# A second block inversion emitted in pieces among the joins and scan steps, and two kinds of stores issued by GpSimd

## The chip, the cores and the metric

The kernel runs on one core of a Trainium2 chip. A core has five engines that run their own instruction streams in order: TensorE (PE in the profile; its weight loads are PEld), VectorE (DVE), ScalarE (ACT), GpSimd (POOL) and SyncE (SP), which here does nothing but issue transfers. Transfers run on the core's 16 DMA engines whichever engine issues them. The metric is the device time of one execution in microseconds (us), and lower is better.

## The reference

One layer of a bidirectional encoder is applied to two sequences of 1024 and 256 tokens, with width 1024 and all in float32. Three groups of heads read one projection of the normalised input: six heads of a gated delta rule, six of retention, four of window attention. The part that the change touches is the delta rule, run once forwards and once backwards in time, in chunks of 64 tokens:

```python
a_mat = jnp.einsum('nbhcd,nbhsd->nbhcs', k_beta, k) * gamma
t_mat = jnp.where(strict, a_mat, 0.0) + jnp.eye(CHUNK, dtype=q.dtype)
rhs = jnp.concatenate([v * beta[..., None], k_beta * jnp.exp(decay)[..., None]], axis=-1)
sol = lax.linalg.triangular_solve(t_mat, rhs, left_side=True, lower=True, unit_diagonal=True)
...
def step(state, inp):
    u_c, w_c, qk_c, qd_c, kd_c, cd_c = inp
    v_new = u_c - jnp.einsum('bhcd,bhde->bhce', w_c, state)
    o = jnp.einsum('bhcd,bhde->bhce', qd_c, state) + jnp.einsum('bhcs,bhse->bhce', qk_c, v_new)
    state = state * cd_c + jnp.einsum('bhcd,bhce->bhde', kd_c, v_new)
    return state, o
```

Each chunk and head needs the inverse of a 64x64 unit triangular matrix; then a scan carries a 64x64 state per head from chunk to chunk.

## The kernel before

The 1280 tokens are 10 blocks of 128, that is 20 chunks of 64. The program runs in five stages; the first and the last are not touched.

1. Load and normalise the input, project the delta rule's queries and keys, convolve them (up to about 180 us).
2. **Preparation** (`prep_stream`, L584 to L643). It walks the blocks from 9 down to 0, and each block has two halves, d = 0 and 1 for the two directions. A half loads a small table `dj` (L606, issued by GpSimd), multiplies it with `sd` on TensorE (L610), exponentiates on ScalarE (`ge`, L613 and L616), and multiplies the products of keys and queries (`gram`, in the two `sa` buffers of PSUM) by it on VectorE: the matrix to invert (`at`, L624) and the step's three matrices (`l2`, printed as `l`, L626 to L628). GpSimd copies a column (`elc`, L629). Then come stores to DRAM: four of `agd` (L631), one of `ad` (L633), and four of `l2d` (L635 and, three times, L638). The next half's `dj` is loaded one block ahead.
3. **Inversion** (`invert(g)`, L402 to L429). Group 1 holds blocks 9 to 5 and is done first; group 0 holds blocks 4 to 0. Two loads (L405) bring the group's 32x32 diagonal blocks, 120 of them per direction, into rows 0 and 1 of the tile `ot`; one long product on VectorE (L414, 120x2048, printed `ot<-ot`) and 60 short ones (L423, L424) invert them all at once; two stores of `yd` (L429), in pieces of 32 numbers, bring them out. Both groups use the same two rows of `ot`, so group 0 can be loaded when group 1 is stored.
4. **Joins and scan** (`scan_stream`, L767 to L791). A `join` (L668) loads two 32x32 inverses (`yn`) and the block between them (`an`), multiplies them on TensorE and stores the 64x64 inverse; there are four for each group. Steps of the scan (L711) follow, one per chunk and direction; the four joins of group 0 come at step 2 (`JN`).
5. In the meantime `fill` (L1107) brings attention, retention and further products of the input with the weights to TensorE.

A weight product is emitted in pieces of 512, 512 and 256 tokens (`dense`, L174), 24 matmuls each: 8 blocks of width times three terms of a split into two parts. During preparation 13 of these products are spread among its halves by weight: `spread` (L443) advances the stream that is behind in proportion to its length. During stage 4 `weave` (L431) does the same by the numbers that the streams yield. Eight of the products are gates (L469): their piece goes through a copy (`sz`) and three more operations on ScalarE and one on VectorE (`sg`), and six of them are stored by SyncE (`gd`, L477), with one buffer for each of the two tiles.

What the streams emit is only a wish. The framework's scheduler simulates the engines and sets the order on each from the order of emission and what is ready there. So a change of emission moves instructions on all engines, far from the lines that changed. On the chip each engine then follows its order strictly; an instruction that waits holds all behind it.

Of the kernel before, what the change touches and what calls it, by code (L numbers as in the profile page):

```python
# [36 lines left out]
PP = ["x0", "x1", "x2", 6, 7, 3, "cq0", "cq1", "ck", "cv", 4, 0, 5]  # L37
PB = [1, 2, "q0"]
RS = [["k0", "v0"], ["q1"], ["k1", "v1"], ["k2"], ["v2"], ["q2"], []]
T_PREP = 10.0  # L40
# [13 lines left out]
def encoder_kernel(ctx: ExitStack, tc: tile.TileContext, I, O, dbg=None, upto=99):  # L54
    nc = tc.nc
# [32 lines left out]
    def tt(eng, out, a, b, op):  # L88
        eng.tensor_tensor(out=out, in0=a, in1=b, op=op)  # L89
# [30 lines left out]
    ot = big.tile([128, 8, PADW], F32, tag="OT", name="ot")  # L120
# [257 lines left out]
    L2D = [[tc.dram_tile([2, 128, 3, 3, 64], F32, name=f"l2d{d}_{b}") for b in range(NB)] for d in range(2)]  # L378
# [3 lines left out]
    YDD = [[tc.dram_tile([120, 32, 32], F32, name=f"yd{d}_{g}") for g in range(2)] for d in range(2)]  # L382
# [5 lines left out]
    T, B = slice(0, 64), slice(64, 128)  # L388
# [11 lines left out]
    IREG = (0, 1)  # L400

    def invert(g):  # L402
        for d in range(2):
            with tc.high_priority():
                nc.sync.dma_start(out=ot[0:120, IREG[d], 0:1056].rearrange("p (a b) -> p a b", a=32),  # L405
                                  in_=AGD[d][g].rearrange("q c p r x -> (q c p) r x"))

        def two(o0, o1, *dims):

            a = ot[0:120, IREG[0], o0:o0 + 1]  # L410
            return bass.AP(a.tensor, a.offset, [list(a.ap[0]), [(IREG[1] - IREG[0]) * PADW + o1 - o0, 2], *([list(e) for e in dims])])

        y, yd = two(0, 0, (33, 32), (1, 32)), two(32, 32, (0, 32), (33, 32))
        tt(V, y, y, yd, MUL)  # L414
        yield 4.2
        for s in range(1, 31):
            na, nb = s, 31 - s
            t3 = two(1056, 1056, (nb, na), (1, nb))

            c = two(s, 33 * (32 - s) + 31 - s, (33, na), (0, nb))  # L420
            r = two(33 * s + s + 1, 33 * (31 - s), (0, na), (1, nb))
            o = two(s + 1, 33 * (32 - s), (33, na), (1, nb))
            tt(V, t3, c, r, MUL)  # L423
            tt(V, o, o, t3, ADD)  # L424
            if s % 3 == 0:
                yield 2.8
        V.memset(two(0, 0, (34, 32)), 1.0)
        for d in range(2):
            nc.sync.dma_start(out=YDD[d][g], in_=ot[0:120, IREG[d], 0:1056].rearrange("p (a b) -> p a b", a=32)[:, :, 0:32])  # L429

    def weave(*run):  # L431

# [10 lines left out]
    def spread(*run):  # L443

        run = [[0.0, t, g] for t, g in run]
        while run:
            q = min(run, key=lambda e: e[0])
            t = next(q[2], None)
            if t is None:
                run.remove(q)  # L450
            else:
                q[0] += t / q[1]
                yield t

    def length(ns):
        return 12.8 * len(ns) or 1.0, prods(*ns)
# [48 lines left out]
    with tc.tile_pool(name="pa", reuse_waits="tile", bufs=2) as pa:  # L505
# [78 lines left out]
        def prep_stream():  # L584
            for b in reversed(range(NB)):
# [18 lines left out]
                for d in range(2):  # L604
# [25 lines left out]
                    for q in range(4):  # L630
                        nc.sync.dma_start(out=AGD[d][b // 5][q, 2 * b % 10:2 * b % 10 + 2].rearrange("c p r x -> r (c p) x"),  # L631
                                          in_=at[32 * q:32 * q + 32, :, :, q % 2, :].rearrange("r c p x -> r (c p) x"))
                    nc.sync.dma_start(out=ADD_[d][b // 5][2 * b % 10:2 * b % 10 + 2].rearrange("c p q w t -> p c q w t"), in_=at)  # L633

                    nc.sync.dma_start(out=L2D[d][b][:, T].rearrange("r p a q t -> p r (a q t)"),  # L635
                                      in_=l2[T].rearrange("p r a q t -> p r (a q t)"))
                    for a, a2 in ((0, 1), (1, 0), (2, 2)):
                        nc.sync.dma_start(out=L2D[d][b][:, B, a2].rearrange("r p q t -> p r (q t)"),  # L638
                                          in_=l2[B, :, a].rearrange("p r q t -> p r (q t)"))
                    yield T_PREP / 2  # L640
                if b % 5 == 0:
                    assert "x2" in gone
                    yield from invert(b // 5)  # L643


        for _ in spread((10 * T_PREP + 2 * 32.2, prep_stream()), length(PP)):
            pass
    if upto <= 3:
        if dbg:
# [117 lines left out]
    def scan_stream():  # L767

        run = [list(range(16, 20)) + list(range(16)), list(range(15, -1, -1)) + list(range(19, 15, -1))]
        for d, cc in ((1, 5), (0, 5), (1, 0), (0, 0)):  # L770
            join(1, d, cc)
            yield T_JOIN
        done = {b: max(run[d].index(2 * b + r) for d in range(2) for r in range(2)) for b in range(NB)}
        for i in range(NC):
            if i == JN:
                for d, cc in ((0, 0), (1, 5), (0, 5), (1, 0)):
                    join(0, d, cc)
                    yield T_JOIN
                inv_cm.__exit__(None, None, None)
            for d in range(2):  # L780
                c = run[d][i]
                ends = (15, 19) if d == 0 else (0, 16)
                step(d, c, c in ((0, 16), (15, 19))[d], c in ends)
            yield T_STEP
            for b in FO:
                if done[b] == i - FD:
                    norm(b)
        for b in FO:
            if done[b] > NC - 1 - FD:
                norm(b)  # L790
        sp_cm.__exit__(None, None, None)  # L791
# [360 lines left out]
    with tc.tile_pool(name="fw", reuse_waits="tile", bufs=2) as fw:  # L1152
# [21 lines left out]
        for gi in range(2):  # L1174
            c0 = WSEQ[gi][1]
            w = wf.pop()
            for i, b in enumerate(range(NB) if gi else FO):
                tk = slice(b * 128, (b + 1) * 128)
                p = acc()
# [22 lines left out]
        for gi in range(2):  # L1202
# [10 lines left out]
            for b in range(NB):  # L1213
                tk = slice(b * 128, (b + 1) * 128)
                end = gi == 1 and b == NB - 1
                for j, (o, n) in enumerate(((0, 256), (256, 256)) if end else ((0, 512),)):
                    cs = slice(o, o + n)
                    p = acc()
# [50 lines left out]
```

## Time and profile before

| What | Value |
|---|---|
| Median of 3 runs | 1094.68 us (1089.72 to 1098.46) |
| Profiled execution, its own time | 1089.4 us |
| Its span | 1087.7 us |
| TensorE busy | 1012.3 us, 93% of the span |
| VectorE / ScalarE / GpSimd busy | 626.2 / 513.4 / 237.1 us |
| Transfers issued by SyncE | 118.97 MB |
| Transfers issued by GpSimd | 0.27 MB |

The busy share of an engine says that it had an instruction running. The granted clock of TensorE (PEclk) is the mean share of full speed; it is below 1 for some microseconds after TensorE sat idle, so that a stop costs its own length and a part of the work behind it. In timelines a bracket behind a row gives the engine's idle time just ahead of it, and what ended it. SPq rows are SyncE's issues of transfers; their time is how long the issue held the queue, not how long the data took.

### The profile page before, as it was taken

Reading aid. Unit: us, or ns where it says so; the run is one execution under the profiler, and the core shown is the slowest. Engines: PE = TensorE matmul, PEld = TensorE weight load, DVE = VectorE, ACT = ScalarE, POOL = GpSimd, SP = SyncE. Lnnn points to the kernel's source line nnn. Section 1 sums busy time; section 2 is a strip of 40 time slices with the busy share of each in tenths; the row PEclk is TensorE's granted clock in tenths of the full one; section 3 lists DMA queues with packets and bytes.
Section 4 is the critical chain, followed back from the end, with each engine's and each line's share of the span. In section 5 each row is a group of like instructions: output and inputs, shape, how many; then the busy total and the mean of one; then the engine's idle time right before and its main releaser. Section 6 shows DMA issues by size and latency. Waiting matters only on the chain.

```text
span 1087.7 us, 20998 instructions
## 1 busy us (share of the span) xinstructions
PE 1012.3 (93%) x7859; PEld 807.6 (74%) x7859; DVE 626.2 (58%) x1303; ACT 513.4 (47%) x1194; POOL 237.1 (22%) x406
## 2 busy tenths in 40 slices
PE   4999999999896799899998999989789999999996
PEld 4768878887785677677776777767567888888885
DVE  6666676754895985555555664575884333412333
ACT  8476779775454554444344322323341121534544
POOL 2001001111212210312323324554451000112311
PEclk9999999999898899999999899989989999999998
DMA  8112112777778336535544434464572530300211
GB/s 258 37 44 69 45 39 58 170 170 180 164 184 173 104 88 131 146 77 137 127 112 109 113 84 116 115 189 113 155 231 65 172 100 1 97 1 10 98 78 77
DMA packets 199071, 120.57 MB, mean 111 GB/s; under 512 B 105906, under 2 KB 180442, under 8 KB 198970
## 3 DMA queue, kind: packets, MB, share of 16 engines
q1 hardware_dynamic: 194074, 118.97, 40.9%
q8 instruction: 62, 1.02, 0.4%
q0 software_dynamic: 4896, 0.27, 0.4%
q14 instruction: 39, 0.32, 0.1%
HBM read 76.26 MB, written 42.91 MB: 110 GB/s over the span
## 4 chain that ended last, share of the span: by engine, by line
PE 72%; DMA 9%; DVE 8%; issue 3%; ACT 3%; SPq 3%; POOL 2%; DVEq 0%; POOLq 0%; ACTq 0%
PE mm L86 42%; PE sa L86 15%; PE sb L86 8%; PE tr L86 4%; DVE ot L984 2%; PE tr L866 1%; DMA xt<-in_x_prompt 1%; DMA ot<-agd 1%; POOL oo L89 1%; DMA oo<-od 1%; DMA agd<-at 1%; DMA raw<-in_w_in 1%; DMA vt<-vtd 1%; PE tr L1191 1%; SPq L638 1%
## 5 line engine op out<-in xcount | busy, mean ns | idle before, releaser
L86 PE MATMUL mm<-xh,whi 128*128 128x512 f32 x720 | 266.7, 370 | 5.0 <-ACT ot L526 1.8
L86 PE MATMUL mm<-xl,whi 128*128 128x512 f32 x720 | 263.3, 366 | 0.0
L86 PE MATMUL mm<-xh,wlo 128*128 128x512 f32 x720 | 263.2, 366 | 0.0
L86 PEld LDWEIGHTS mm<-xh,whi 128*128 128x128 f32 x720 | 138.5, 192 | 30.3 <-ACT ot L526 2.9
L86 PEld LDWEIGHTS mm<-xh,wlo 128*128 128x128 f32 x720 | 138.1, 192 | 22.2 <-issue 1.0
L86 PEld LDWEIGHTS mm<-xl,whi 128*128 128x128 f32 x720 | 138.4, 192 | 20.4 <-issue 0.7
L89 DVE TENSOR_TENSOR ot<-ot 128x1284 f32<-128x1284 f32 (+16 forms) x131 | 85.0, 649 | 28.7 <-ACT ot L102 16.2
L89 DVE TENSOR_TENSOR wlo<-raw,whi 128x1024 fp32r<-128x1024 f32 (+1 forms) x56 | 56.7, 1015 | 39.0 <-ACT whi L149 26.2
L86 PE MATMUL mm<-whi,xh 128*128 128x512 f32 (+1 forms) x168 | 66.6, 398 | 1.3 <-ACT xh L1056 1.3
L86 PE MATMUL mm<-whi,xl 128*128 128x512 f32 (+1 forms) x168 | 66.0, 393 | 0.4 <-DVE xl L89 0.4
L86 PE MATMUL mm<-wlo,xh 128*128 128x512 f32 (+1 forms) x168 | 65.9, 392 | 0.0
L86 PE MATMUL sa<-wlo,xh 128*128 128x512 f32 (+1 forms) x160 | 62.7, 392 | 0.0
L86 PE MATMUL sa<-whi,xl 128*128 128x512 f32 (+1 forms) x160 | 62.6, 391 | 0.0
L86 PE MATMUL sa<-whi,xh 128*128 128x512 f32 (+1 forms) x160 | 62.5, 390 | 0.0
L531 DVE SCALAR_TENSOR_TENSOR ot<-ot,cols 128x1284 f32<-128x1284 f32 x36 | 55.9, 1553 | 0.5
L89 DVE TENSOR_TENSOR sgm<-sb,sgm 128x512 f32<-128x512 f32 (+1 forms) x21 | 14.0, 666 | 72.5 <-ACT sgm L102 60.3
L86 PE MATMUL sa<-sv,l 128*64 128x64 f32 (+1 forms) x912 | 45.8, 234 | 4.2 <-DVE sv L748 3.3
L89 POOL TENSOR_TENSOR sv<-sv,elc 64x192 f32<-64x192 f32 x72 | 41.5, 576 | 37.2 <-PE sa L86 22.2
L86 PEld LDWEIGHTS sa<-sv,l 128*64 128x64 f32 (+1 forms) x912 | 35.5, 141 | 16.0 <-issue 5.1
L89 POOL TENSOR_TENSOR ot<-ot,sgm 128x512 f32<-128x512 f32 x19 | 25.4, 1339 | 99.5 <-DVE sgm L89 98.1
L89 POOL TENSOR_TENSOR vt<-vt,sab 128x192 f32<-128x192 f32 x40 | 21.7, 547 | 115.6 <-DMA vt<-vtd 107.0
L149 ACT CAST whi<-raw 128x1024 fp32r<-128x1024 f32 x30 | 31.5, 1050 | 16.9 <-PE mm L86 10.8
(302 smaller groups left out, 1967.2 us busy)
## 6 DMA issues: line engine op xcount, KB each, us to landing
raw<-in_w_in SPq DMA_DIRECT2D x28, 512.0 KB, 4.3
l<-l2d SPq DMA_DIRECT2D x40, 288.0 KB, 2.9
l2d<-l SPq DMA_DIRECT2D x60, 96.0 KB, 2.8
l2d<-l SPq DMA_DIRECT2D x20, 288.0 KB, 3.7
xt<-in_x_prompt SPq DMA_DIRECT2D x8, 512.0 KB, 6.8
ot<-in_x_prompt SPq DMA_DIRECT2D x8, 512.0 KB
raw<-in_w_pg SPq DMA_DIRECT2D x16, 256.0 KB, 3.1
yp<-ot SPq DMA_DIRECT2D x8, 512.0 KB, 2.6
```

Of the source, the lines that this page charges most:

```text
L86: nc.tensor.matmul(out, lhsT, rhs, start=start, stop=stop)
L89: eng.tensor_tensor(out=out, in0=a, in1=b, op=op)
L149: S.copy(hi, raw)
L531: V.scalar_tensor_tensor(out=Y[:, 0:1284], in0=R[:, j:j + 1284], scalar=cw(ti, j), in1=Y[:, 0:1284], op0=MUL, op1=ADD)
L638: nc.sync.dma_start(out=L2D[d][b][:, B, a2].rearrange("r p q t -> p r (q t)"), in_=l2[B, :, a].rearrange("p r q t -> p r (q t)"))
L866: nc.tensor.transpose(pt[:, k * 128:(k + 1) * 128], pr[:, k * 128:(k + 1) * 128], ident)
L984: V.scalar_tensor_tensor(out=st[r, b2, h], in0=st[r, b, h], scalar=gs[r, 2 * p + h:2 * p + h + 1], in1=kvt[r, b, h], op0=MUL, op1=ADD)
L1191: nc.tensor.transpose(pt[:, k * 128:(k + 1) * 128], hb[:, b, (n * 4 + k) * 128:(n * 4 + k + 1) * 128], ident)
```

## The change

Three things change, and nothing that is computed does.

First, `invert(0)` leaves the preparation stream. `scan_stream` now holds it as a generator: after each of the four joins of group 1 it takes two pieces of it (a piece is three of the 30 double steps; the first is the long product), and before the joins of group 0 it takes the rest. The weights of `spread` follow: the preparation counts 132.2 instead of 164.4 units, so that the 13 products are spread over the preparation alone.

Second, the stores of the inverses `yd` (two per group, 480 KB each) are issued by GpSimd instead of SyncE.

Third, the stores of the step's matrices `l2d` (four per half block, 80 in all, 96 or 288 KB each) are issued by GpSimd too.

```diff
         for d in range(2):
-            nc.sync.dma_start(out=YDD[d][g], in_=ot[0:120, IREG[d], 0:1056].rearrange("p (a b) -> p a b", a=32)[:, :, 0:32])
+            nc.gpsimd.dma_start(out=YDD[d][g], in_=ot[0:120, IREG[d], 0:1056].rearrange("p (a b) -> p a b", a=32)[:, :, 0:32])
...
-                    nc.sync.dma_start(out=L2D[d][b][:, T].rearrange("r p a q t -> p r (a q t)"),
+                    nc.gpsimd.dma_start(out=L2D[d][b][:, T].rearrange("r p a q t -> p r (a q t)"),
                                       in_=l2[T].rearrange("p r a q t -> p r (a q t)"))
                     for a, a2 in ((0, 1), (1, 0), (2, 2)):
-                        nc.sync.dma_start(out=L2D[d][b][:, B, a2].rearrange("r p q t -> p r (q t)"),
+                        nc.gpsimd.dma_start(out=L2D[d][b][:, B, a2].rearrange("r p q t -> p r (q t)"),
                                           in_=l2[B, :, a].rearrange("p r q t -> p r (q t)"))
                     yield T_PREP / 2
-                if b % 5 == 0:
+                if b == 5:
                     assert "x2" in gone
-                    yield from invert(b // 5)
+                    yield from invert(1)
...
-        for _ in spread((10 * T_PREP + 2 * 32.2, prep_stream()), length(PP)):
+        for _ in spread((10 * T_PREP + 32.2, prep_stream()), length(PP)):
             pass
...
         run = [list(range(16, 20)) + list(range(16)), list(range(15, -1, -1)) + list(range(19, 15, -1))]
+        inv0 = invert(0)
         for d, cc in ((1, 5), (0, 5), (1, 0), (0, 0)):
             join(1, d, cc)
             yield T_JOIN
+            for _ in range(2):
+                next(inv0)
         done = {b: max(run[d].index(2 * b + r) for d in range(2) for r in range(2)) for b in range(NB)}
         for i in range(NC):
             if i == JN:
+                for _ in inv0:
+                    pass
                 for d, cc in ((0, 0), (1, 5), (0, 5), (1, 0)):
                     join(0, d, cc)
```

The order that the scheduler makes of it is shown at three places. In the rows, the number behind a name is the buffer's; lines behind L767 stand five lower in the changed kernel.

**Place 1, group 1's inversion.** VectorE's order where that inversion begins. `at` and `l` are block 4's, second half (in the first listing) and first half (in the second); `sa` are the block's two buffers of products in PSUM, which TensorE fills anew for block 3 when they are read. Before:

```order
L89 TENSOR_TENSOR l_295_2640<-kq,ge_2627 128x2x192
L89 TENSOR_TENSOR ot<-ot 120x2x32x32
L89 TENSOR_TENSOR ot<-ot 120x2x30 x2
L89 TENSOR_TENSOR at_2698<-sa_2602,ge_2686 128x6x32
L89 TENSOR_TENSOR l_301_2699<-sa_2602,ge_2686 128x192
L89 TENSOR_TENSOR ot<-ot 120x2x58
L89 TENSOR_TENSOR at_2698<-sa_2609,ge_2686 128x6x32
L89 TENSOR_TENSOR l_301_2699<-sa_2609,ge_2686 128x192
```

In the changed kernel the long product 32x32 stands 24 rows ahead of the first of these:

```order
L89 TENSOR_TENSOR ot<-ot 120x2x12x19
L89 TENSOR_TENSOR at_2781<-sa_2744,ge_2769 128x6x32
L89 TENSOR_TENSOR l_306_2782<-sa_2744,ge_2769 128x192
L89 TENSOR_TENSOR ot<-ot 120x2x234
L89 TENSOR_TENSOR at_2781<-sa_2751,ge_2769 128x6x32
L89 TENSOR_TENSOR l_306_2782<-sa_2751,ge_2769 128x192
L89 TENSOR_TENSOR l_306_2782<-kq,ge_2769 128x2x192
L89 TENSOR_TENSOR ot<-ot 120x2x13x18
```

Before, block 4's first half came ahead of the inversion and its second half right behind the long product; now both halves stand in the middle of it, between the 24th and the 34th of its 60 short products. TensorE's order moved with it: between the last `sb<-dj` of block 5 and the products of block 3 it now has 120 product matmuls of 512 columns and 67 of 256.

**Place 2, the end of preparation.** SyncE's order, before:

```order
L638 DMA l2d_0_387<-l_381_3346 64x2x192
L429 DMA yd_1_406<-ot 3840x1x32
L429 DMA yd_1_408<-ot 3840x1x32
L638 DMA l2d_0_387<-l_381_3346 64x2x192 x2
L138 DMA raw_3574<-in_w_in 128x8x128
L405 DMA ot<-agd_0_401 120x1056
L477 DMA gd_449<-sg_3389 128x512
L405 DMA ot<-agd_0_403 120x1056
```

and in the changed kernel:

```order
L631 DMA agd_0_401<-at_3522 32x6x33 x4
L477 DMA gd_447<-sg_3438 128x256
L633 DMA ad_0_397<-at_3522 128x2x198
L405 DMA ot<-agd_0_401 120x1056
L631 DMA agd_0_403<-at_3588 32x6x33 x4
L633 DMA ad_0_399<-at_3588 128x2x198
L477 DMA gd_450<-sg_3477 128x512
L405 DMA ot<-agd_0_403 120x1056
```

The loads of group 0 (`ot<-agd_0`) now follow their own stores with one gate's store between. VectorE's order there, in the changed kernel, where `kst` and `qlz` are what attention's first matmuls read:

```order
L89 TENSOR_TENSOR sg_3566<-sg_3566,sz_3567 128x512
L89 TENSOR_TENSOR ot<-ot 120x2x32x32
L817 TENSOR_SCALAR snk<-rvb 128x1 x4
L823 TENSOR_SCALAR qlz_3687<-ident 64x256 x2
L89 TENSOR_TENSOR kst_3657<-ot,kst_3657 64x512
L811 CAST bias<-iot 128x384
L89 TENSOR_TENSOR kst_3658<-ot,kst_3658 64x512
```

Before, the long product stood behind all of `kst` and `qlz`; now it stands ahead of them. TensorE's order between the last `sb<-dj` and the first matmul that reads `kst` holds three product pieces less three matmuls (24 of 256 columns, 45 of 512), where it held four (24 of 256, 72 of 512) before.

**Place 3, GpSimd's order where group 1's inverses are stored.** `dj` is the table of the half one block later. Before, there are no stores in it:

```order
L629 COPY elc<-ge_2947 128x6
L606 DMA dj_456<-drd_376 2x6x64 x2
L629 COPY elc<-ge_3006 128x6
L606 DMA dj_455<-drd_375 2x6x64 x2
L629 COPY elc<-ge_3088 128x6
```

and in the changed kernel:

```order
L629 COPY elc<-ge_3001 128x6
L638 DMA l2d_3_390<-l_332_3014 64x2x192 x2
L635 DMA l2d_3_390<-l_332_3014 64x2x576
L638 DMA l2d_3_390<-l_332_3014 64x2x192
L429 DMA yd_1_406<-ot 3840x1x32
L429 DMA yd_1_408<-ot 3840x1x32
L606 DMA dj_455<-drd_375 2x6x64 x2
L629 COPY elc<-ge_3122 128x6
```

Each half's four stores, and here the two of the inverses, now stand ahead of a load of `dj`. The stores of group 0's inverses stand in GpSimd's order among the scan's operations (`sv`, `vt`) and attention's casts (`qh`).

## The prediction

> **What bounds the kernel now.** I read the windows by stage first, to see where TensorE loses time. Columns: stretch, its length, busy us (and instructions) of PE, PEld, DVE, ACT and POOL, granted clock, DMA share, GB/s.
>
> ```profile
> 250.00:285.00 35.00, 30.02 (x183) 25.48 (x182) 22.51 (x52) 17.59 (x62) 7.34 (x16) 0.90 0.67 152
> 285.00:345.00 60.00, 59.59 (x355) 49.63 (x354) 48.47 (x106) 31.73 (x89) 8.51 (x22) 1.00 0.80 178
> 345.00:375.00 30.00, 15.87 (x159) 13.50 (x160) 22.04 (x50) 12.32 (x29) 8.92 (x14) 0.77 0.57 147
> 375.00:435.00 60.00, 59.62 (x619) 47.92 (x619) 44.66 (x94) 32.59 (x65) 5.59 (x6) 1.00 0.43 102
> 435.00:450.00 15.00, 10.76 (x118) 8.57 (x117) 8.95 (x24) 5.43 (x16) 5.07 (x8) 0.89 0.66 170
> 450.00:575.00 125.00, 125.00 (x1586) 97.91 (x1586) 70.47 (x213) 52.10 (x138) 31.13 (x52) 1.00 0.46 114
> 575.00:625.00 50.00, 42.60 (x515) 33.21 (x513) 30.29 (x97) 21.44 (x67) 17.88 (x45) 0.90 0.43 111
> ```
>
> In the stages that the change touches TensorE is the bound, with three holes: 5 us around 270, 14.1 us from 345 (30.00 less 15.87), 4.2 us at 435. Nothing else can be won there, since the matmuls stay the same. PE's timeline gives each hole (start, length, what, idle time before it and what ended it):
>
> ```profile
> 275.09 2.83 PE L86 MATMUL sa<-kq 64*64 64x128 f32 x24 [4.23 <-DVE l L89]
> 358.40 0.55 PE L86 MATMUL sb<-kst,qh 128*128 128x256 f32 x1 [13.07 <-DVE mx L852]
> 439.98 0.58 PE L86 MATMUL sb<-kst,qh 128*128 128x384 f32 x1 [4.24 <-DVE mx L852]
> ```
>
> The clock drops behind each. In finer windows:
>
> ```profile
> 275.00:280.00 5.00, 4.91 (x34) 4.58 (x35) 4.79 (x16) 3.18 (x11) 1.09 (x2) 0.53 0.34 77
> 355.00:360.00 5.00, 1.60 (x7) 1.63 (x8) 5.00 (x13) 1.14 (x4) 3.87 (x4) 0.50 0.81 252
> 360.00:365.00 5.00, 4.45 (x83) 4.20 (x81) 4.76 (x14) 4.81 (x12) 1.86 (x4) 0.84 0.00 1
> 440.00:445.00 5.00, 5.00 (x19) 3.86 (x20) 3.53 (x8) 2.83 (x9) 3.18 (x7) 0.66 0.54 177
> ```
>
> Busy time times the missing clock: 4.91 x 0.47 = 2.3 us; 1.60 x 0.50 + 4.45 x 0.16 = 1.5 us; 5.00 x 0.34 = 1.7 us. So the holes cost 6.5, 15.6 and 5.9 us.
>
> Why VectorE was late stands in its own timeline and in SyncE's:
>
> ```profile
> 269.98 4.38 DVE L89 TENSOR_TENSOR ot<-ot 120x2048 f32<-120x2048 f32 x3 [3.17 <-DMA ot<-agd]
> 326.66 0.35 DVE L89 TENSOR_TENSOR at<-sa,ge 128x192 f32<-128x192 f32 x1
> 352.09 3.82 DVE L89 TENSOR_TENSOR ot<-ot 120x2048 f32<-120x2048 f32 x1 [6.87 <-DMA an<-ad]
> 438.59 0.68 DVE L682 STREAM_TRANSPOSE xn<-yn 128x480 f32<-128x480 f32 x1 [4.78 <-DMA yn<-yd]
> ```
>
> ```profile
> 327.04 1.78 SPq L631 DMA_DIRECT2D agd<-at  x4
> 331.62 5.63 SPq L429 DMA_DIRECT2D yd<-ot  x2
> 337.30 4.88 SPq L638 DMA_DIRECT2D l2d<-l  x2
> 342.93 0.59 SPq L405 DMA_DIRECT2D ot<-agd  x1
> 344.07 0.50 SPq L405 DMA_DIRECT2D ot<-agd  x1
> ...
> 418.52 5.04 SPq L429 DMA_DIRECT2D yd<-ot  x2
> 423.65 4.35 SPq L477 DMA_DIRECT2D gd<-sg  x1
> 435.42 0.52 SPq L678 DMA_DIRECT2D yn<-yd  x1
> ```
>
> All three are one pattern: VectorE stands at an operation that waits for a load, and what TensorE needs stands behind it. In the second hole group 0's load goes out at 344.07, though its matrices left SyncE at 328.82; two inverse stores and two matrix stores held the queue in between. The long product then runs from 352.09 to 355.91, and the row that names `an` as its releaser means this load. In the third hole the last `yn` load leaves at 435.42 because inverse stores and the gate's store behind them held SyncE from 418.52 to 428.00.
>
> **The change part by part.** *Group 1's inversion (place 1).* Before, block 3's products waited for reads of block 4 that stood behind the long product. Now TensorE has 120 x 0.234 + 67 x 0.118 = 36 us of product matmuls there, and with the preparation's own about 41 us. The two spacings are from these rows, half of 0.235 for 256 columns:
>
> ```profile
> 343.85 0.40 PE L86 MATMUL mm<-xl,whi 128*128 128x512 f32 x1
> 344.08 0.39 PE L86 MATMUL mm<-xh,wlo 128*128 128x512 f32 x1
> ...
> L89 DVE TENSOR_TENSOR ot<-ot x61: 222/542/3865, 270.0 to 330.6; 120x60 f32<-120x60 f32 x4, 120x116 f32<-120x116 f32 x4, 120x168 f32<-120x168 f32 x4, 120x216 f32<-120x216 f32 x4
> ```
>
> VectorE's side: from the `dj` matmul to the data in `ot` I take 14 us (worked out below, at place 2), then the long product 3.8, 33 short ones at the group's median of 0.542 = 17.9, and some 5 us for the eleven other operations among them (0.35 for an `at`): 40.7 us. That is just inside 41, and an upper bound, since operations overlap at their ends (the row at 269.98 has three in 4.38 us, the first of them a long product). I count the hole as gone: -6.5 us; if it stays by a few microseconds, half of that.
>
> *End of preparation (place 2).* From the last `sb<-dj` matmul (323.47, 0.52 for two) to `at` done at 327.01 is 3.5 us. The stores take 1.8 to issue and land in 3.1; the load takes 0.4 to issue and lands in 5.3:
>
> ```profile
> 337.41 0.33 DVE L812 TENSOR_SCALAR snk<-rvb 128x1 f32<-128x1 f32 x4
> 340.71 0.69 DVE L89 TENSOR_TENSOR kst<-ot,kst 64x512 fp32r<-64x512 f32 x1
> ...
> 323.47 0.52 PE L86 MATMUL sb<-dj,sd 128*128 128x384 f32 x2
> agd<-at SPq DMA_DIRECT2D x80, 24.8 KB, 3.1
> ot<-agd SPq DMA_DIRECT2D x4, 495.0 KB, 5.3
> ```
>
> So the data are there after 14.1 us, and the long product is done after 18. `snk`, `qlz`, `bias` and the first two `kst` took from 337.41 to 341.40 in the old order, 1.3 of it idle, so TensorE's first `kst` matmul starts after 20.7. The four other `kst`, two `qlz` and the gate's product free the next piece after another 4.8 or so (seven operations of the 0.69 us size), at 25.5. TensorE's cover is now 45 x 0.234 + 24 x 0.118 = 13.4 us, against 19.7 before, and 1.5 us of matmuls lie in the wait. Idle: 25.5 - 13.4 - 1.5 = 10.6, and some 2 us until the gate's chain has freed a PSUM buffer: 12.6 against 14.1. SyncE saves about ten microseconds, and the new order gives most of it back, since the long product stands ahead of `kst` and the cover is shorter. -1.5 us, the clock's loss as before; bounds 0 and -15.6.
>
> The Trainium skill ("DMA: Bandwidth & Descriptors", section "Issuing engines are not separate DMA queues") says that transfers of all issuing engines run on the same 16 DMA engines, and that a second issuer saves no more than the issue time, which is usually small. The rows above show issue times of 5.6 and 4.9 us with VectorE waiting, so here it is not small; by the rule alone, with no credit for the reordering at place 1, the sum below would be about -4.4.
>
> *Third hole.* With `yd` off SyncE the `yn` load can leave some 9 us earlier, ahead of 435.6, when TensorE stopped: -5.9 us.
>
> *What is added to GpSimd.* 80 matrix stores and 4 inverse stores. What it issues today:
>
> ```profile
> L606 POOL DMA_DIRECT2D dj<-drd x40: 548/548/597, 98.7 to 309.1; - x40
> dj<-drd POOLq DMA_DIRECT2D x40, 3.0 KB, 3.3
> L374 POOL DMA_DIRECT2D drd<-dr x2: 535/542/549, 96.2 to 103.2; - x2
> L429 SPq DMA_DIRECT2D yd<-ot x4: 932/2524/4580, 331.6 to 419.5; - x4
> ...
> 302.07 1.09 POOL L606 DMA_DIRECT2D dj<-drd  x2 [1.50 <-PE sb L86]
> 308.51 1.09 POOL L606 DMA_DIRECT2D dj<-drd  x2 [1.64 <-PE sb L86]
> ```
>
> A load of 12 rows and a store of 60 cost the same 0.55 us. At that price a half block adds 2.2 us to GpSimd's 1.1, in a period of 6.4 us (302.07 to 308.51): it fits, and the matrices are only read in the scan. The inverse store has 3840 rows, and no row here shows such a one on GpSimd. Below, it costs 0.55; above, if the 0.542 of 60 rows were all price per row, 64 times that, 35 us. I take SyncE's 2.5 us for the same transfer, the nearest row. At that price nothing waits: the `dj` pair behind it lands 4.4 us after its issue begins (1.09 and 3.3) and is used a block later, 12.9 us, so 8.5 us are spare for two stores.
>
> *The inversion's pieces.* They ran beside attention before, too; now they also run beside the scan's first two steps. Each VectorE operation there (`sv` copies and sums, four dependent links in two steps) finds one or two pieces ahead of it, 0.5 to 1.3 us. TensorE's products cover some: between 0 and 6 us, I take 3.
>
> Sum: -6.5 - 1.5 - 5.9 + 3 = -10.9 us. Against the profiled execution that is 1089.4 - 10.9 = 1078.5; that execution is as fast as the fastest of the three runs, so I take the sum off their median: 1094.68 - 10.9 = 1083.8. From 575 us on both programs have nearly the same order, so what is won stays won.
>
> **The rivals.** *A, the second hole closes too.* The load goes out soon enough for TensorE not to run dry: -6.5 - 15.6 - 5.9 + 3 = -25, 1069.7 us. For it: SyncE's ten microseconds. Against it: VectorE's order at place 2. Chance 0.12.
>
> *B, the gain is waited away.* If the scan's chain and not TensorE sets the pace from 575 us on (7.4 us idle, clock 0.90), TensorE only arrives earlier at the same waits: about 1092. Against it, 125 of 125 us busy from 450 to 575. The same time results if the holes merely move. Chance 0.20.
>
> *C, slower: the inverse store's price on GpSimd.* Two stores of price P stand ahead of `dj` in the preparation and ahead of casts and state products in the scan. From P of about 4.2 us the spare 8.5 us are used up, and each store pair then costs 2P - 8.5. At P = 10: 2 x 11.5 = 23 us against 13.9 - 3 won, +12, 1107. For it: 3840 short rows generated by an engine that has done 60 at most; against it, the flat price so far. The Trainium skill ("SBUF — State Buffer", section "SBUF: two separate sides") adds that GpSimd cannot write a transfer's descriptors while VectorE runs an operation that takes both SBUF ports. The 40 `dj` issues took 548 to 597 ns in a stretch with VectorE at 48.47 of 60 us, so the trace shows no such stall at this size. Chance 0.11. *D, slower for another reason*, by 5 to 20 us: the scan's early steps, now closer to each other in TensorE's order, wait for their loads. Chance 0.07.
>
> **How the numbers follow.** My forecast has 0.50. One per cent, about what a measurement of this kernel can tell from none, is 10.9 us, so the forecast, give or take 5 us, lies half on either side of it. Faster by over 1%: 0.25 + 0.12 of A + 0.05 of B, where a part is kept, = 0.42. Within 1%: 0.25 + 0.13 of B + 0.03 of C and D = 0.41. Slower: 0.17 with B's rest. The range, 1068 to 1102, holds the forecast, most of A, B, and C up to P of about 8.
>
> **What would show it.** Right: no wait of the products `sa<-kq` on `l` near 270; group 0's loads issued within about 9 us of the last `sb<-dj`; a hole of 10 to 13 us before attention's matmuls with `kst`, ended by `kst` or the gate's copy; none at the third join; GpSimd's `yd` near 2.5 us. Wrong: `yd` on GpSimd above 4 us with `dj` late behind it, a hole of 4 us or more between 400 and 575, or more than 8 us of idle time where there were 7.4 from 575 on.

## The result and the profile after

The changed kernel takes **1112.24 us** (median of 4 runs, 1109.38 to 1113.56), the kernel before 1094.24 us on the same chip: a ratio of 1.0156 with a 95% interval of 1.0116 to 1.0196. It is slower by 18 us, where 1084 was forecast and 1068 to 1102 given as the range.

The profiled execution took 1113.56 us with a span of 1111.8, 24.1 us more than before. The page of the changed kernel, its engines:

```profile
span 1111.8 us, 21067 instructions
PE 1027.6 (92%) x7859; PEld 818.2 (74%) x7859; DVE 630.7 (57%) x1303; ACT 512.1 (46%) x1194; POOL 287.9 (26%) x490
```

TensorE does the same matmuls as before, but is busy for 1027.6 us against 1012.3: 15.3 us more, nearly all of it lower clock. Its idle time is 84.2 us against 75.4: 8.8 more. Together these are the 24.1. The same stretches as in the prediction, with one ahead of them that was full before (70.00 of 70 us busy):

```profile
180.00:250.00 70.00, 65.55 (x396) 54.66 (x395) 38.82 (x77) 49.93 (x125) 25.26 (x47) 0.98 0.65 143
250.00:285.00 35.00, 32.96 (x183) 27.36 (x182) 18.27 (x37) 15.83 (x49) 10.89 (x20) 0.95 0.63 154
285.00:345.00 60.00, 55.97 (x331) 46.34 (x330) 42.13 (x89) 22.45 (x65) 23.90 (x41) 0.94 0.59 122
345.00:375.00 30.00, 24.06 (x127) 19.32 (x128) 8.61 (x20) 16.24 (x49) 8.77 (x17) 0.94 0.61 155
375.00:435.00 60.00, 47.55 (x320) 38.34 (x319) 44.87 (x101) 31.96 (x71) 18.01 (x31) 0.86 0.54 136
435.00:450.00 15.00, 15.00 (x185) 12.04 (x185) 12.83 (x28) 8.58 (x21) 0.79 (x2) 1.00 0.46 111
450.00:575.00 125.00, 122.58 (x1627) 97.00 (x1625) 81.75 (x209) 49.24 (x122) 34.04 (x47) 0.99 0.49 113
575.00:625.00 50.00, 44.86 (x633) 33.49 (x631) 36.29 (x129) 25.66 (x84) 18.45 (x45) 0.93 0.52 134
```

The three holes of before, 24.1 us of idle time between 180 and 575 with the crumbs, have become 31.3 us spread over nearly every stretch. Most of the long ones, in PE's timeline:

```profile
221.82 0.39 PE L86 MATMUL mm<-xh,whi 128*128 128x256 f32 x1 [2.28 <-ACT sz L473]
...
301.63 0.79 PE L86 MATMUL mm<-xh,whi 128*128 128x512 f32 x1 [4.03 <-ACT ot L393]
...
355.91 0.44 PE L832 MATMUL tr<-ident,ot 128*128 128x128 f32 x2 [2.36 <-ACT kc L603]
...
385.98 0.79 PE L86 MATMUL mm<-xh,whi 128*128 128x512 f32 x1 [4.83 <-ACT sz L473]
...
397.62 0.79 PE L86 MATMUL mm<-xh,whi 128*128 128x512 f32 x1 [4.23 <-ACT sz L473]
...
408.62 0.39 PE L86 MATMUL mm<-xh,whi 128*128 128x256 f32 x1 [1.55 <-ACT sz L473]
...
416.31 0.50 PE L86 MATMUL mm<-xh,whi 128*128 128x512 f32 x1 [1.12 <-ACT sz L473]
```

The waits on `l` at 275 and on `mx` at 358 and 440 are gone. In their place TensorE waits for ScalarE. The first row of TensorE's waits in the changed kernel (total us, times, longest):

```profile
PE mm L86 <- ACT sz L473: 17.6, 9, 4.8
```

and two of ScalarE's:

```profile
ACT at L622 <- DMA ad<-at: 44.1, 13, 11.5
...
ACT sg L100 <- DMA gd<-sg: 28.6, 11, 5.9
```

Before, TensorE's wait was 1.1 us, and ScalarE's waits for the `ad` store 19.1, between 180 and 450 us:

```profile
ACT sg L100 <- DMA gd<-sg: 34.7, 14, 8.0
ACT at L622 <- DMA ad<-at: 19.1, 10, 4.5
```

A "per cent" below is the ratio to the kernel before, run beside it, with its 95% interval; a few executions took far longer, up to 1895 us, and the ratios leave these out.

### The profile page after: what moved, and what is told of

Read it like the earlier page. It is cut to its first block, busy times and chain, and to the rows that moved or that the text cites. A ratio compares the mean times of both kernels' runs of the same rounds, so it can differ in the third digit from the quotient of the medians.

```text
span 1111.8 us, 21067 instructions
## 1 busy us (share of the span) xinstructions
PE 1027.6 (92%) x7859; PEld 818.2 (74%) x7859; DVE 630.7 (57%) x1303; ACT 512.1 (46%) x1194; POOL 287.9 (26%) x490
## 4 chain that ended last, share of the span: by engine, by line
PE 65%; DMA 11%; DVE 9%; ACT 5%; issue 4%; SPq 4%; POOL 1%; DVEq 0%; ACTq 0%; POOLq 0%
PE mm L86 37%; PE sa L86 15%; PE sb L86 7%; PE tr L86 4%; DMA gd<-sg 3%; DMA ad<-at 2%; DVE ot L89 2%; DVE ot L989 1%; SPq L631 1%; PE tr L871 1%; DMA od<-os 1%; DMA xt<-in_x_prompt 1%; PE tr L1196 1%; DVE l L89 1%; DMA oo<-od 1%
## 5 line engine op out<-in xcount | busy, mean ns | idle before, releaser
L86 PE MATMUL mm<-xh,whi 128*128 128x512 f32 x720 | 271.4, 377 | 24.7 <-ACT sz L473 17.6
L86 PE MATMUL mm<-xl,whi 128*128 128x512 f32 x720 | 267.6, 372 | 0.0
L86 PE MATMUL mm<-xh,wlo 128*128 128x512 f32 x720 | 267.1, 371 | 0.0
L86 PEld LDWEIGHTS mm<-xh,whi 128*128 128x128 f32 x720 | 141.6, 197 | 52.2 <-ACT sz L473 20.1
L86 PEld LDWEIGHTS mm<-xh,wlo 128*128 128x128 f32 x720 | 141.5, 197 | 21.9 <-issue 0.7
L86 PEld LDWEIGHTS mm<-xl,whi 128*128 128x128 f32 x720 | 141.6, 197 | 21.1 <-issue 1.0
L89 DVE TENSOR_TENSOR wlo<-raw,whi 128x1024 fp32r<-128x1024 f32 (+1 forms) x56 | 56.2, 1005 | 31.3 <-ACT whi L149 16.7
L89 POOL TENSOR_TENSOR sv<-sv,elc 64x192 f32<-64x192 f32 x72 | 39.2, 545 | 41.5 <-PE sa L86 23.5
L638 POOL DMA_DIRECT2D l2d<-l x60 | 36.3, 607 | 16.6 <-DVE l L89 15.8
```

Source lines behind the costliest of these rows:

```text
L86: nc.tensor.matmul(out, lhsT, rhs, start=start, stop=stop)
L638: nc.gpsimd.dma_start(out=L2D[d][b][:, B, a2].rearrange("r p q t -> p r (q t)"), in_=l2[B, :, a].rearrange("p r q t -> p r (q t)"))
```

## The experiments: each part alone, and taken back

My first theories were W (the weight: 13 products, six of them gates, with one buffer for each tile, are pressed into a preparation that counts 132.2 instead of 164.4; the expectation below says eight gates, which is the count of the whole kernel), S (the stores issued by GpSimd run in the same microseconds as SyncE's) and R (no single cause: the order before is a lucky one).

**stores_only**: both kinds of stores on GpSimd, nothing else.

```diff
-nc.sync.dma_start(out=YDD[d][g], ...    -nc.sync.dma_start(out=L2D[d][b] ...
+nc.gpsimd.dma_start(out=YDD[d][g], ...  +nc.gpsimd.dma_start(out=L2D[d][b] ...
```

> The kernel before with both kinds of stores on GpSimd; the inversion of group 0 and the weights stay as they were. Theory W (the weights: 13 products, eight of them gates with one buffer each, are squeezed into a preparation that counts 132.2 instead of 164.4, and the gates' chain of copy, three operations, product and store becomes the bound): TensorE's waits for the gate's copy stay near 1 us and the time at or a little under the kernel before, 1085 to 1096. Theory S (the stores that GpSimd issues run in the same microseconds as those of SyncE, so that the gate's stores and the diagonal blocks' stores land late): the gate's stores land in over 4 us as in the changed kernel, and the time is 1102 to 1112.

**inversion_only**: the changed kernel with `nc.sync` at those stores.

> The changed kernel with both kinds of stores back on SyncE, so the inversion in pieces and the weights alone. Theory W: most of the loss is here, 1103 to 1112, with over 12 us of TensorE's waits for the gate's copy. Theory S: 1085 to 1097, the gate's stores land in about 2.6 us.

**old_weight**: the changed kernel with one number back.

```diff
-        for _ in spread((10 * T_PREP + 32.2, prep_stream()), length(PP)):
+        for _ in spread((10 * T_PREP + 2 * 32.2, prep_stream()), length(PP)):
```

> The changed kernel with the preparation counted as 164.4 in the spread, as before; everything else changed. Theory W: the products are spread wider, waits for the gate's copy fall from 17.6 to under 6 us, and the time to 1085 to 1097. Theory S: still 1106 to 1114.

**l2d_on_sync**: the changed kernel with the `l2d` stores alone back on `nc.sync`.

> The changed kernel with the matrix stores back on SyncE; GpSimd keeps the four inverse stores. Theory S (80 matrix stores on a second queue): 1088 to 1098 and the gate's stores land in about 2.6 us. Theory W: 1104 to 1114, no better than the changed kernel, as the gate's chain is as crowded.

**weight_only**: the kernel before with `10 * T_PREP + 32.2` in that line, nothing else.

> The kernel before with one number changed: the preparation counts 132.2 in the spread, so the 13 products come earlier and closer; inversion and stores as before. Theory W (the squeezed gates): TensorE's waits for the gate's copy rise from 1.1 us to over 8, and the time to 1102 to 1112. Theory R (no single cause: the order before is a favourable one, and any other costs about one per cent): also about 1105, but without waits for the gate's copy above 4 us. Neither: 1090 to 1098.

**yd_only**: the kernel before with the four `yd` stores on GpSimd.

> The kernel before with only the four inverse stores on GpSimd. My own prediction's part of it (SyncE's queue is freed of 5.6 us ahead of group 0's load, and the third hole closes): 1083 to 1090. Theory S, if the inverse stores and not the matrix stores are what hurts: 1102 to 1110 with the joins' loads of inverses landing late. Theory R: about 1105 with holes at other places.

**nudge**: the kernel before with `10 * T_PREP + 2 * 32.2 + 4`.

> The kernel before with the preparation counted as 168.4 in the spread where it was 164.4: the stores, the inversion and the amount of work are unchanged, a few product pieces come a little later, and the order on the engines shifts in many rows. Theory R (any order but the one before costs about one per cent): 1102 to 1110. Against it: 1090 to 1099.

| Kernel | us | Ratio | 95% interval | ScalarE waits for `ad`, us |
|---|---|---|---|---|
| stores_only | 1107.59 | 1.0107 | 1.0074 to 1.0141 | 53.4 |
| inversion_only | 1108.52 | 1.0123 | 1.0070 to 1.0176 | 47.2 |
| old_weight | 1104.03 | 1.0088 | 1.0049 to 1.0127 | 43.9 |
| l2d_on_sync | 1114.50 | 1.0174 | 1.0138 to 1.0211 | 51.1 |
| weight_only | 1108.55 | 1.0122 | 1.0068 to 1.0175 | 35.9 |
| yd_only | 1093.56 | 0.9980 | 0.9954 to 1.0005 | 29.0 |
| nudge | 1100.82 | 1.0028 | 1.0004 to 1.0053 | 22.9 |

Neither W nor S alone holds: each part made alone costs more than 1%. weight_only and inversion_only cost the same, so of that part it seems to be the one number in `spread` that costs, and not the inversion that is moved; both_undone below confirms it. yd_only costs nothing, so of the stores it is `l2d`. The two prices don't add up: 1.2 and 1.1 make 1.6, and with the new weight, `l2d` back on SyncE brings nothing. (inversion_only differs from l2d_on_sync by the inverse stores alone; the intervals overlap, so whether these cost anything beside the new weight is open.) R is not borne out: the nudge put thousands of TensorE's matmuls in another order and cost 0.3%, between what R and its opposite had expected. A difference of that size can therefore come from the order alone. old_weight did what W expected of the waits (2.6 us for the gate's copy), but not of the time. yd_only closed the third hole (0.8 us idle between 380 and 440, where there were 4.6) without the gain that my prediction gave that part.

## The experiments: what the weight costs

**no_gate_chain** and **no_gate_chain_before**: the gates' function left out, in the changed kernel and in the kernel before.

```diff
-                S.copy(zt, pp[:, :w])
-                sigmoid(sg, zt)
-                tt(V, sg, sg, zt, MUL)
+                S.copy(sg, pp[:, :w])
```

> The changed kernel without the gates' function: the gate's product is copied straight to the stored tile, and the three operations of ScalarE and the product on VectorE are left out, so that the gates' values are not those of the reference. It takes the gates' chain away. Theory W: the waits of 17.6 us and their loss of clock go, 1078 to 1092. Theories S and R: the time falls by no more than the same edit saves in the kernel before, and stays above 1100.

> The kernel before with the same part left out (the gates' function; the values are not those of the reference): the measure for the run above. TensorE waits 1.1 us for the gate's copy there, so theory W expects 1085 to 1096; theory R expects anything up to 1107, since the order on all engines changes with it.

Measured: 1098.64 us (1.0035, 1.0014 to 1.0057), between what the theories expected, and for the kernel before 0.9888 (0.9842 to 0.9933). The edit takes 1.2 per cent off the changed kernel and 1.1 off the kernel before, with some half a per cent of doubt. So the gates' chain isn't what tells the two apart, although the largest row of waits named it. With it gone, another wait for ScalarE stood first, in the waits of no_gate_chain:

```profile
PE mm L86 <- ACT ot L393: 9.7, 4, 4.4
...
PE mm L86 <- ACT sg L472: 8.1, 3, 4.2
```

The next theories were A (ScalarE's copy into `at`, which has two buffers, waits for the store of two halves ago) and C (the products that come early are missing as cover later on, whoever waits).

**at3_after, at3_before, at3_stores**: `AB = 3` for `AB = 2` in the changed kernel, the kernel before and stores_only.

> The changed kernel with three buffers for the matrix to invert instead of two. Theory A (ScalarE stands at the copy into that tile until the store of two halves ago has landed, 44.1 us in the changed kernel against 19.1 before; the exponentials, the evacuations and the gates' copies stand behind it, and TensorE behind those): the waits fall under 15 us and the time to 1090 to 1100. Theory C (the products that came early are missing as cover of the second inversion, whoever waits): 1105 to 1113, with 10 us or more of idle TensorE around group 0's inversion still there.

> The kernel before with three buffers for that tile, the measure for the run above. TensorE had no idle time from 180 to 250 us and 0.4 us from 285 to 325, so theory A expects little: 1088 to 1097.

> Both kinds of stores on GpSimd, inversion and weights as before (stores_only, 1107.59 us, 53.4 us of ScalarE's waits for that landing), with three buffers. Theory A: the 13.5 us that were lost between 180 and 325 go, 1092 to 1099. If the matrix stores hurt in another way (late loads of dj, queues): 1103 to 1109 still.

Measured: at3_after 1.0174 (1.0145 to 1.0202), at3_before 0.9987 (0.9971 to 1.0004), at3_stores 1.0046 (1.0029 to 1.0063). In at3_after nothing is won. at3_stores came down by 0.6%, but its waits did not: 51.8 us against 53.4 in stores_only, since the scheduler moved the copies forward in ScalarE's order by as much as the third buffer allowed. So theory A is not shown, and what brought at3_stores down stays open.

**weight_two_later** is weight_only with the last two products emitted with attention's; **two_later** is the same edit in the changed kernel:

```diff
-PP = ["x0", "x1", "x2", 6, 7, 3, "cq0", "cq1", "ck", "cv", 4, 0, 5]
-PB = [1, 2, "q0"]
+PP = ["x0", "x1", "x2", 6, 7, 3, "cq0", "cq1", "ck", "cv", 4]
+PB = [0, 5, 1, 2, "q0"]
```

> weight_only (1108.55 us: only the number 132.2 changed) with the same two products emitted with attention's. Theory C: 1092 to 1099, near the kernel before, since only the place of two products differs. Otherwise 1104 or more.

> The changed kernel with the last two products of the preparation (gates 0 and 5) emitted with attention's instead, so that 11 products are spread over 132.2, about the density of 13 over 164.4 before. Theory C (cover: the products that came early are missing when TensorE waits for group 0's inversion, attention's first operands and the joins): idle time and loss of clock between 325 and 475 us fall by 8 us or more, and the time to 1094 to 1103. If the weight costs in another way: still 1107 or more.

Measured: weight_two_later 1101.33 us, 1.0042 (1.0018 to 1.0067), two thirds of the weight's price back by the place of two products, though 2 us more than theory C expected. The last matmul that reads `dj`, which ends preparation for TensorE, starts at 323.7 us before, at 362.3 in weight_only and at 331.9 in weight_two_later. The first waits of TensorE in weight_only and in weight_two_later, without those of the first stage:

```profile
PE mm L86 <- ACT sz L473: 11.9, 6, 3.6
...
PE sb L86 <- ACT qh L842: 6.8, 1, 6.8
PE sb L86 <- DVE qlz L89: 6.3, 1, 6.3
```

```profile
PE sb L86 <- DVE qlz L89: 13.5, 1, 13.5
...
PE mm L86 <- ACT sz L473: 6.3, 3, 2.5
```

With the small number the products come so densely that TensorE waits 11.9 us for ScalarE's copies of gates, where the kernel before has 1.1. And the hole at the end of preparation is still there (6.8 and 6.3), with fewer products left to fill it. Up to 450 us it is there that weight_only loses its time (some more is lost behind 575). From 180 to 325 us TensorE is idle for 5.3 us in it and for 5.4 before. From 325 to 450 it is idle for 24.8 us at a clock of 0.88, in weight_only, against 18.8 at 0.93 before:

```profile
325.00:450.00 125.00, 100.23 (x791) 80.30 (x791) 82.64 (x176) 63.50 (x154) 22.28 (x36) 0.88 0.55 133
```

```profile
325.00:450.00 125.00, 106.25 (x997) 86.76 (x996) 89.33 (x202) 62.08 (x132) 22.25 (x35) 0.93 0.55 130
```

With two products later the waits for copies of gates are about halved, and the hole is one piece. two_later, with the `l2d` stores still on GpSimd, took 1111.42 us, 1.0127 (1.0092 to 1.0162), where theory C expected 1103 at most: by itself this edit doesn't mend the changed kernel.

## The experiments: what the matrix stores cost

Theory O came out of the rows. In stores_only, GpSimd issues the matrix stores of a half block while SyncE is still busy with the stores of `at`. Timelines of GpSimd, SyncE and ScalarE in stores_only:

```profile
209.45 1.23 POOL L638 DMA_DIRECT2D l2d<-l  x2 [0.51 <-DVE l L89]
210.66 0.59 POOL L635 DMA_DIRECT2D l2d<-l  x1
211.25 0.59 POOL L638 DMA_DIRECT2D l2d<-l  x1
...
211.16 0.44 SPq L633 DMA_DIRECT2D ad<-at  x1
...
216.81 0.21 ACT L622 COPY at<-nbeta 128x12 f32<-128x12 f32 x1 [2.90 <-DMA ad<-at]
```

and SyncE and ScalarE in the kernel before:

```profile
221.91 0.44 SPq L633 DMA_DIRECT2D ad<-at  x1
222.45 0.58 SPq L635 DMA_DIRECT2D l2d<-l  x1
...
224.76 0.22 ACT L622 COPY at<-nbeta 128x12 f32<-128x12 f32 x1 [0.43 <-DMA ad<-at]
```

From the issue of `ad` to the copy that waits for it: 5.65 us in the first, 2.85 in the second. (These are stores of different half blocks; the store of the same half as the second took 4.10 us in stores_only.) SyncE's queue had kept an order that nobody had written down as one: first the stores that ScalarE waits for, then the matrices that are read only in the scan. Over all such waits between 180 and 400 us the median of this time is 4.6 to 5.4 us in six kernels with `l2d` on GpSimd (4.59 in stores_only, 4.86 in the changed one), and 3.5 to 4.0 in thirteen with `l2d` on SyncE (3.51 before).

**l2d_first** reverses that order on SyncE alone: the four `l2d` stores of a half are emitted ahead of its `agd` and `ad`.

> The kernel before, all stores on SyncE, but the four matrix stores of a half block are emitted ahead of its five stores of the matrix to invert. Theory O (order of the transfers: with l2d on GpSimd the matrix stores leave beside or ahead of the ad store, on whose landing ScalarE's next copy waits; the ad store then took 4.4 to 5.2 us from its issue to that copy, in five kernels, against 3.3 to 4.0 in the eight with l2d on SyncE): ScalarE's waits for ad rise from 19.1 us to over 40, and the time to 1102 to 1112. If it is GpSimd itself (the late dj loads, its slower landing): 1092 to 1100.

Measured: 1101.68 us, 1.0055 (1.0032 to 1.0079). The first of ScalarE's waits:

```profile
ACT at L622 <- DMA ad<-at: 44.0, 14, 6.8
```

and the stretch that was full before:

```profile
180.00:250.00 70.00, 65.25 (x411) 54.08 (x410) 40.41 (x81) 50.32 (x128) 9.75 (x23) 0.98 0.66 143
```

The same stretch in stores_only:

```profile
180.00:250.00 70.00, 65.39 (x393) 54.15 (x393) 38.22 (x77) 48.93 (x123) 27.54 (x52) 0.95 0.65 141
```

The waits came as theory O expected, and TensorE lost 4.75 us in that stretch as it had lost 4.61 in stores_only, with GpSimd not taking part. (From the issue of `ad` to the copy the median is 3.93 us here, the upper end; so the delay must lie mostly ahead of it, where `ad` is issued behind the matrices.) The time rose to just under what theory O had expected, by half of what stores_only lost. So matrices that go ahead of `ad` are shown to bring the waits and the loss in that stretch. That the same holds in stores_only, where `ad` isn't issued later but lands later, is argued from it. The size is uncertain: 0.55% is not far above the 0.3% of the nudge, which touched no store. What the rest is (GpSimd's own later issues, or where the scheduler then put things) stays open.

## The experiments: both mended

**both_undone** is the changed kernel with the weight of 164.4 and `l2d` on SyncE; **two_later_l2d_sync** is two_later with `l2d` on SyncE; **yd_at3** is yd_only with `AB = 3`.

> The changed kernel with the preparation counted as 164.4 and the matrix stores back on SyncE: what is left of the change is the inversion in pieces and the four inverse stores on GpSimd. If the weight and the matrix stores hold the whole loss: 1088 to 1098, ScalarE's waits for ad under 32 us. If the moved inversion itself costs (its pieces beside the scan's first steps): 1102 or more.

> The changed kernel with gates 0 and 5 emitted with attention's products and the matrix stores on SyncE; inversion in pieces, the weight of 132.2 and the inverse stores on GpSimd stay. If both mended parts hold the loss: 1092 to 1102 (weight_two_later gave 1101.33). If the two causes are not what is shown: 1108 or more, as with l2d_on_sync.

> The kernel before with the four inverse stores on GpSimd and three buffers for the matrix to invert. Alone they gave 0.998 and 0.9987; together 0.996 to 1.000, 1090 to 1096, not to be told from the kernel before at one per cent.

Measured: both_undone 1096.06 us, 0.9990 (0.9968 to 1.0012); two_later_l2d_sync 1091.92, 0.9946 (0.9919 to 0.9972); yd_at3 0.9949 (0.9922 to 0.9976). All kernels with the moved inversion and the inverse stores on GpSimd, in one table:

| | weight 164.4 | weight 132.2 | 132.2, two products later |
|---|---|---|---|
| `l2d` on SyncE | 0.9990 | 1.0174 | 0.9946 |
| `l2d` on GpSimd | 1.0088 | 1.0156 (the changed kernel) | 1.0127 |

The weight and the matrix stores hold the whole loss; what is left without them is no slower than before. In the first and the third column `l2d` on GpSimd costs 1.0 and 1.8%. In the middle one it costs nothing, perhaps since the crowded products make ScalarE late in any case; that this is why the prices don't add up is argued, not shown. two_later_l2d_sync and yd_at3 beat the kernel before by half a per cent, and so the changed one by two. In two_later_l2d_sync the gain is not where it was forecast: TensorE still waits at both first holes.

```profile
PE sb L86 <- ACT qh L847: 10.4, 1, 10.4
PE sb L86 <- DVE qlz L89: 8.2, 1, 8.2
...
PE sa L86 <- DVE l L89: 4.1, 1, 4.1
```

## Why the prediction was wrong

Three steps failed. At place 1 the sum followed VectorE's results to TensorE, but not to ScalarE, which also waits for them, through a store. At place 2 the clock's loss was mis-sized. And the matrix stores on GpSimd were put at nothing.

*Group 1's inversion (place 1), forecast -6.5 us: the wait on `l` went, another came.* No wait on `l` is left, and the 36 us of product matmuls do stand there. But with block 4's halves in the middle of the inversion the matrix `at` is stored late, too, and ScalarE stands at its next copy into that tile until the store has landed. The evacuation that TensorE waited for at 301.63 stands right behind. SyncE and ScalarE in the changed kernel:

```profile
296.28 0.53 SPq L633 DMA_DIRECT2D ad<-at  x1
...
300.89 0.21 ACT L622 COPY at<-nbeta 128x12 f32<-128x12 f32 x1 [11.54 <-DMA ad<-at]
```

So a stop of 4.03 us with 2.7 us of clock took the place of one of 4.23 with 2.3. The longest such wait of ScalarE before was 4.5 us. The step that failed is to count the products as cover for the path over `l` and `sa` alone, and to count them as a gift. They are the same 13 products, spread over the halves and one inversion where there were two, and the sum has no term for the stretches from 180 to 345 us, which were full (1.2 us idle outside the hole at 270: 4.98 less 4.23, and 0.41). They now idle for 4.45, 2.04 and 4.03 us, nearly all of it for ScalarE (`ot` 4.0, `sz` 3.2, `ge` 3.2). With the clock the terms left 1.4 us to be lost from 180 to 345, and 15.8 are lost. ScalarE is not too busy for it: from 285 to 345 it is busy for 22.45 us, less than the 31.73 before. It stands, 37.3 us for `ad` alone from 180 to 345, in place of 19.1. Which part of the change brings how much here is not separated: the new weight and the matrix stores each cost TensorE some of the first stretch, 3.4 us in weight_only and 4.61 in stores_only.

*End of preparation (place 2), forecast 12.6 us idle and 1.5 of clock: the length was right by luck, the shape was wrong.* The last `sb<-dj` and group 0's loads, timelines of PE and SyncE in the changed kernel:

```profile
377.56 0.42 PE L86 MATMUL sb<-dj,sd 128*128 128x384 f32 x1
```

```profile
379.66 0.35 SPq L405 DMA_DIRECT2D ot<-agd  x1
...
386.96 0.46 SPq L405 DMA_DIRECT2D ot<-agd  x1
```

The loads went out 2.1 and 9.4 us behind, as listed, and from 375 to 435 TensorE was idle for 12.45 us. But I had 10.6 us of it wait for `kst` and 2 for the gates' chain. The first matmul with `kst` didn't wait at all, and 11.7 us went to the gates' copies: 4.83, 4.23, 1.55 and 1.12. For the second of these ScalarE itself stood until the gate's store of the piece before, issued at 385.25, had landed:

```profile
391.84 0.63 ACT L100 ACTIVATE sg<-sz 128x512 f32<-128x512 f32 x1 [5.91 <-DMA gd<-sg]
```

So the wait is cut by pieces of products that stood in its way, and the clock drops behind each stop. Finer windows, changed kernel:

```profile
385.00:390.00 5.00, 4.02 (x11) 3.25 (x12) 1.45 (x2) 0.92 (x2) 2.27 (x4) 0.66 0.94 231
395.00:400.00 5.00, 2.38 (x6) 1.90 (x7) 4.94 (x8) 4.60 (x11) 0.26 (x1) 0.63 0.48 101
400.00:405.00 5.00, 5.00 (x17) 3.96 (x16) 4.84 (x6) 0.00 (x0) 2.70 (x2) 0.69 0.85 230
410.00:415.00 5.00, 4.65 (x78) 4.45 (x77) 4.17 (x16) 3.80 (x9) 0.99 (x3) 0.67 0.00 0
415.00:420.00 5.00, 3.88 (x23) 2.98 (x17) 4.88 (x14) 3.50 (x10) 0.00 (x0) 0.67 0.33 79
```

Busy time times the missing clock: 1.4 + 0.9 + 1.5 + 1.5 + 1.3 = 6.6 us. "The clock's loss as before" is the failed step here: it was mis-sized by 5.1 us.

*Third hole, forecast -5.9: nearly right.* The loads of the fourth join now go out from 464 to 467 us, ahead of group 0's inverse stores at 478. Behind them TensorE waits for 0.94 us, where it waited for 4.24:

```profile
473.02 0.44 PE L86 MATMUL sb<-kst,qh 128*128 128x384 f32 x1 [0.94 <-DVE mx L857]
```

*What is added to GpSimd, forecast 0: the prices were right, and a bearer of the cost was missed.* An inverse store took 1.78 us to issue, a matrix store 0.6, and no `dj` load held TensorE. (One of them, at 343.24, stood on GpSimd for 5.86 us until an inverse store had landed, a wait that the price by issue time doesn't hold.) "It fits, and the matrices are only read in the scan" is the failed step: it asks whether GpSimd has time and who reads the matrices, not which stores they now run beside or ahead of. stores_only and yd_only show that price, 1.1% with `l2d` moved and none without, and l2d_first that such an order alone brings the waits. The rule that I had weighed says this too: the Trainium skill ("DMA: Bandwidth & Descriptors", section "Issuing engines are not separate DMA queues") has transfers of all issuers on the same 16 engines interleave with each other. I had used its other half, on issue time. The traces fit it: from the issue of `ad` to the copy 4.59 us in stores_only against 3.51 before, in the median.

*The inversion's pieces, +3, bounds 0 and 6: not measured alone.* both_undone holds them together with the inverse stores on GpSimd and is at 0.9990, with yd_only, which holds those stores alone, at 0.9980. So they cost no more than a few microseconds.

*"What is won stays won" from 575 on: not quite.* TensorE's idle time from there to the end is 35.4 us against 34.7, but windows of 5 us give a loss of clock of 18.4 against 14.0.

Altogether, in windows of 5 us, 180 to 575 loses 46.4 us of TensorE's time where it lost 29.9, idle time and clock together: +16.5 where the terms said -10.9. Behind 575 the same count gives 5.1 more, ahead of 180 0.9; the rest of the 24.1 these windows don't place.

*The rivals.* Of the two on the slower side, C asked for an inverse store above 4.2 us on GpSimd; it took 1.78. D fell too: the longest wait of TensorE for a load in the whole scan was 1.0 us. B's condition, a scan that sets the pace from 575, did not decide. That the packing of products or the order of stores costs was among none of them.

*The signs.* The signs of being right that I had listed nearly all came: no wait on `l`, the loads within some 9 us, 12.45 us of idle time at place 2, hardly a hole at the joins, 1.78 us for an inverse store. Of the signs of being wrong none came: no hole of 4 us or more between 400 and 575, and 5.1 us idle from 575 to 625 where there were 7.4. They watched only the places where the sum had a term.

## What to carry to other kernels

A stretch where TensorE is full is no free room for more of its work: each piece has to be evacuated, and the engine that does so, and what it waits for, must be costed with it. That engine need not be busy to be late; here it stood for stores. When an operation is moved, follow its result to everything that waits for it, through stores and buffers too. A queue that seems too full may also be an order that works: before moving stores to another issuer, ask which of the stores behind or ahead of them somebody waits for. And when a change has several parts, the row with the most waiting time names where it shows, not which part caused it: here the named chain cost both kernels about the same.

## What the runs showed of the hardware

Short stops cost as much clock as a long one, or more. Before, a stop of 13.07 us was followed by 1.5 us lost to a lower clock. In the changed kernel stops of 4.83 and 4.23 us were followed by 1.4 and, in two windows, 2.4 us. Even stops of 1.55 us (at 408.62) and 1.12 (at 416.31), each with a shorter one ahead of it, go with windows at 0.67, which lose 1.5 and 1.3.

A store of 3840 pieces of 128 bytes took GpSimd 1.71 to 1.84 us to issue, steadier than SyncE's 0.93 to 4.58 for the same one:

```profile
L429 POOL DMA_DIRECT2D yd<-ot x4: 1707/1780/1838, 327.3 to 479.9; - x4
```
